# Column pairs 2 and 3 of each FFN's first projection as a Strassen group: ten groups instead of nine

## The chip, the cores and the metric

The kernel runs on one core of one Trainium2 chip. The metric is the device time of one execution in microseconds (us). Before the change three runs gave 1077.87, 1078.4 and 1086.64 us, median 1078.4 us. Stretches of time below are counted from the first instruction of the profiled execution.

## The reference

A two-layer decoder trunk on one sequence of 512 tokens with 1024 channels, all in float32. Each layer is a mixer and then a SwiGLU feed-forward network (FFN), each followed by a residual sum and a layer norm:

```
D_MODEL, SEQ, DEPTH, D_FF = 1024, 512, 2, 2816

def swiglu(x, w_in, w_out):          # w_in 1024 x 5632, w_out 2816 x 1024
    h = x @ w_in
    return (silu(h[..., :D_FF]) * h[..., D_FF:]) @ w_out

for layer in range(DEPTH):
    mix = even_mixer(x, ...) if layer % 2 == 0 else odd_mixer(x, ...)
    x = layer_norm(ALPHA * x + mix, ...)
    x = layer_norm(ALPHA * x + swiglu(x, ffn_w_in[layer], ffn_w_out[layer]), ...)
```

The even mixer is a short gated convolution beside a multi-window pooling, the odd mixer a forgetting attention beside a Conformer convolution; each has one input and one output projection. The change touches the FFN alone.

## The kernel before

**Precision.** Matrices are multiplied in a float32r format. Each operand is split into two: `hi`, a copy in that format made by ScalarE (ACT), and `lo`, the remainder, made by VectorE (DVE) or GpSimd (POOL). A product is then three matmuls, hi·hi, hi·lo and lo·hi (`split` in lines 85 to 88, `mm3` in lines 90 to 93). So every weight block costs a load, one ACT pass and one DVE or POOL pass before TensorE (PE) can use it whole. The activations stand transposed as `xh` and `xl`: 8 blocks of 128 channels by 512 tokens.

**The two forms of the first projection.** Of `w_in`, 22 blocks of 128 gate columns and 22 of 128 up columns are needed. A *plain* block n takes its two column blocks through `project` (lines 151 to 157): 2 column blocks x 8 channel blocks x 3 matmuls of 128x512. `load_cols` fetches 512 KB into a `raw` buffer (3 of them), and hi and lo go into `wt` buffers (8 of them). The blocks n = 0 and 1 (`FIRST = 2`) are loaded together, their lo by POOL, and are computed in two halves of 256 tokens (`SPLIT`), so that the first half runs while the last token blocks are still being normalised. The blocks n = 2 and 3 were plain too (`PLAIN = 4`), each over all 512 tokens.

From column `PLAIN` on, two neighbouring blocks make a *group* (class `Strassen`). It treats channels, tokens and the gate/up choice as 2x2 blocks and needs seven products P1 to P7 instead of eight. A product (lines 383 to 390) is 2 x 4 x 3 = 24 matmuls of 128x256. Its stationary side is a combination of four 512 KB weight quarters `q11, q21, q22, q12`, which `load` (line 364) brings into `wt` buffers in this order; `add` (line 370, DVE) forms the sums S1 to S4; `hi` (line 377, ACT) and `lo` (line 381, DVE) split each of the seven operands into `sw` buffers. The moving side are combinations of the activations that are formed once per FFN.

**`moving`** (lines 319 to 350) forms them on DVE and ACT, outside the fixed part: `less` twice (lines 328 to 330: t3 and t1, each with a help buffer `combl` from `wt`), `minus` twice (lines 334 and 335: t2, t4), and four splits (lines 87 and 88): T2 and T3, t1 back into a block of `xh`/`xl` (so only after the plain matmuls have read that block), and T4. That is ten DVE operations of 128x1024 and four lo's.

**The order in a group** is written by hand (`group`, lines 425 to 485, inside `manual_schedule` for PE, ACT and DVE). PE runs P1, P4 of the group before, P2, P3 of the group before, P6, P5, P7; the first group of a run has no P4 and P3 of another before it. P1 and P2 use `xh`/`xl` as they are, P6 the combination T2, P5 the t1, P7 the T3. `opening` (lines 420 to 423) comes ahead of P1: hi of P1 on ACT, then on DVE the sum S1 = q21 + q22 and only after it the lo of P1. `c1` and `u2`, `u3` (line 397) are copies of PSUM made by ACT. Every wait of an engine holds up what stands behind it on that engine. Outside the hand-written part a scheduler decides the order at build time; the loads all stand on SyncE's (SP) queue in one order, and a load that waits for its buffer holds up those behind it.

**The FFN** (`ffn`, lines 502 to 568): plain blocks, `moving`, the groups up to column 12 (`PART`), the first half of the output projection (`OutProj`), the groups from column 12 to 21 (five of them), and the rest of the output projection with the layer norm. The last group of each run ends in `closing` (lines 487 to 500).

Of the kernel before, what the change touches and what calls it, by code (L numbers as in the profile page):

```python
# [39 lines left out]
FIRSTS = "x0 d1 d2 x1 w0 d3 ww A0 w1 x2 A1 x3 B0 B1 pp"  # L40
SPLIT = [(0, 256), (256, 512)]
FIRST = 2
PLAIN = 4
PART = 12
SHIFT = 16
DFIRST = 2
# [15 lines left out]
def trunk(ctx, tc, x, ev_w_in, ev_conv_w, ev_pool_w, ev_pool_scale, ev_w_out, od_w_in,  # L62
# [131 lines left out]
    def affine_steps(g, b, eng):  # L194

        gb = [wtp.tile([P, D], F32, tag="wt", name="gb") for _ in range(2)]
        for dst, v in zip(gb, (g, b)):
            nc.sync.dma_start(dst, v.partition_broadcast(P))
        return [lambda t=t, cs=slice(c * 512, (c + 1) * 512), v=v, op=op:
                eng.tensor_tensor(xs[t][:, cs], xs[t][:, cs], v[:, cs], op=op)  # L200
                for t in range(NT) for c in range(2) for v, op in zip(gb, (ALU.mult, ALU.add))]
# [300 lines left out]
    def ffn(l):  # L502
        w_in, w_out = ffn_w_in[l], ffn_w_out[l]
        with tc.tile_pool(name=f"ffn{l}", bufs=1) as hp:
# [6 lines left out]
            lhs = lambda k: [y[:, k % 2, :] for y in pairs[k // 2]]  # L511
            for n in range(PLAIN):
                if n < FIRST and n % FIRST == 0:
# [18 lines left out]
            def groups(ns, then=lambda i: None):  # L532

                ns, last = list(ns), None
                load = lambda: st.load(w_in, ns.pop(0), new_pair()) if ns else None
                g = load()
                st.opening(g)
                while g:
                    g, last = st.group(g, last, load, then), g
                st.closing(last)  # L540

            FIXED = {mybir.EngineType.PE, mybir.EngineType.Activation, mybir.EngineType.DVE}
            with tc.manual_schedule(engines=FIXED):
# [5 lines left out]

                groups(range(PLAIN, PART, 2), load_out)  # L550
                steps = affine_steps(ln_mix_g[l], ln_mix_b[l], nc.vector)
# [600 lines left out]
```

## Time and profile before

| | us |
|---|---|
| median of three runs | 1078.4 |
| the profiled execution, its own time | 1077.13 |
| span of the profiled execution | 1075.4 |
| PE busy | 1040.8 |
| DVE busy | 742.5 |
| ACT busy | 482.6 |
| mean granted clock of PE | 0.990 |

The time of the profiled execution is 1.7 us longer than its span. PE is busy in 97% of the span. Rows of the timeline give the start, the length, the engine, the line of the kernel, the operation and its tiles; in square brackets stands how long the engine was idle before and what released it. `x24` means that neighbouring instructions are merged. Matmuls overlap, so that their spacing is read from their starts and not from their lengths.

### The profile page before, as it was taken

The numbers are of one execution on the slowest core, as the hardware profiler recorded it, in microseconds if no ns is written. First come the engines' busy times: TensorE is split into PE (matmuls) and PEld (weight loads), VectorE is DVE, ScalarE is ACT, GpSimd is POOL, SyncE is SP. The second block draws the span as 40 slices with busy tenths as digits, with TensorE's granted clock in tenths as the row PEclk, the third lists the DMA queues.
The fourth block names the chain that finished last, engine by engine and source line by source line (L and its number), as shares of the span: only waits on it lengthen the run. The fifth ranks groups of instructions, "written<-read, shape, count | busy, mean of one in ns | idle before, by whom it ended". The sixth has DMA issues, their size and how long they took to land.

```text
span 1075.4 us, 16367 instructions
## 1 busy us (share of the span) xinstructions
PE 1040.8 (97%) x6649; PEld 934.3 (87%) x6649; DVE 742.5 (69%) x1028; ACT 482.6 (45%) x711; POOL 177.1 (16%) x162
## 2 busy tenths in 40 slices
PE   8999999999799999999999999999999799999997
PEld 8888899899788999988978777889899788999986
DVE  3845476988653788757579978466888663788756
ACT  4433243554321455433576888533555321455420
POOL 1000300000000000012499972710000000000003
PEclk9999999999899999999999999999999899999999
DMA  6523502530423340460333332411530433340522
GB/s 197 148 84 113 157 1 63 174 99 21 157 98 118 119 136 21 137 177 21 80 86 91 96 104 59 121 36 42 183 110 2 163 111 117 118 138 21 164 72 79
DMA packets 112457, 108.49 MB, mean 101 GB/s; under 512 B 5256, under 2 KB 93880, under 8 KB 112382
## 3 DMA queue, kind: packets, MB, share of 16 engines
q1 hardware_dynamic: 110462, 105.35, 31.8%
q10 hardware_dynamic: 1920, 2.10, 0.6%
q8 instruction: 52, 0.85, 0.3%
q14 instruction: 23, 0.19, 0.1%
HBM read 103.17 MB, written 2.10 MB: 98 GB/s over the span
## 4 chain that ended last, share of the span: by engine, by line
PE 76%; DVE 10%; ACT 5%; issue 3%; DMA 2%; POOL 2%; ACTq 0%; SPq 0%; POOLq 0%; DVEq 0%
PE fl L389 13%; PE fl L91 8%; PE fl L93 8%; PE fl L92 8%; PE sc L389 6%; PE sc L93 5%; PE sc L92 5%; PE sc L91 5%; DVE sw L381 4%; DVE sum L370 2%; PE py L92 2%; PE py L91 2%; PE py L93 2%; PE cv L93 2%; PE cv L91 2%
## 5 line engine op out<-in xcount | busy, mean ns | idle before, releaser
L87 ACT ACTIVATE w<-raw 128x1024 fp32r<-128x1024 f32 x104 | 109.4, 1058 | 197.4 <-PE sc L92 64.2
L389 PE MATMUL fl<-T,sw 128*128 128x256 f32 x1296 | 162.0, 281 | 14.2 <-ACT u L397 11.1
L389 PEld LDWEIGHTS fl<-T,sw 128*128 128x128 f32 x1296 | 155.5, 191 | 16.8 <-ACT u L397 12.2
L88 DVE TENSOR_TENSOR w<-raw,w 128x1024 fp32r<-128x1024 f32 x77 | 93.9, 1223 | 84.0 <-ACT w L87 83.4
L88 POOL TENSOR_TENSOR w<-raw,w 128x1024 fp32r<-128x1024 f32 x27 | 64.9, 2415 | 417.9 <-ACT w L87 404.2
L377 ACT ACTIVATE sw<-sum 128x1024 fp32r<-128x1024 f32 x72 | 76.1, 1062 | 102.9 <-DVE sum L370 77.3
L381 DVE TENSOR_TENSOR sw<-sum,sw 128x1024 fp32r<-128x1024 f32 x72 | 87.8, 1219 | 24.7 <-ACT sw L377 24.7
L389 PE MATMUL sc<-xh,sw 128*128 128x256 f32 x576 | 104.5, 277 | 0.0
L389 PEld LDWEIGHTS sc<-xh,sw 128*128 128x128 f32 x576 | 89.7, 188 | 0.1
L381 DVE TENSOR_TENSOR sw<-q,sw 128x1024 fp32r<-128x1024 f32 x54 | 65.4, 1220 | 29.2 <-ACT sw L377 29.1
L389 PE MATMUL sc<-xl,sw 128*128 128x256 f32 x288 | 79.8, 277 | 0.0
L169 POOL TENSOR_TENSOR rs<-rs,neghalf 128x1 f32<-128x1 f32 x20 | 13.6, 678 | 401.8 <-DVE rs L168 401.8
L377 ACT ACTIVATE sw<-q 128x1024 fp32r<-128x1024 f32 x54 | 56.4, 1051 | 44.2 <-DMA q<-in_ffn_w_in 44.2
L91 PE MATMUL fl<-w,hh 128*128 128x512 f32 (+1 forms) x176 | 67.8, 385 | 0.5 <-ACT w L87 0.5
L93 PE MATMUL fl<-w,hl 128*128 128x512 f32 (+1 forms) x176 | 67.6, 384 | 0.0
L92 PE MATMUL fl<-w,hh 128*128 128x512 f32 (+1 forms) x176 | 67.6, 384 | 0.0
L755 DVE SCALAR_TENSOR_TENSOR cv<-hp,par,cv 128x512 f32<-128x512 f32 x84 | 63.1, 751 | 5.8 <-ACT cv L743 4.5
L370 DVE TENSOR_TENSOR sum<-q,q 128x1024 f32<-128x1024 f32 x36 | 43.9, 1218 | 25.5 <-DMA q<-in_ffn_w_in 25.5
L91 PE MATMUL sc<-xh,w 128*128 128x256 f32 (+1 forms) x168 | 55.1, 332 | 0.0
L92 PE MATMUL sc<-xl,w 128*128 128x256 f32 (+1 forms) x168 | 55.0, 329 | 0.0
L389 PE MATMUL fl<-xh,sw 128*128 128x256 f32 x288 | 53.2, 279 | 1.9 <-DVE sw L381 1.9
L93 PE MATMUL sc<-xh,w 128*128 128x256 f32 (+1 forms) x168 | 54.8, 328 | 0.0
(419 smaller groups left out, 2638.8 us busy)
## 6 DMA issues: line engine op xcount, KB each, us to landing
q<-in_ffn_w_in SPq DMA_DIRECT2D x72, 512.0 KB
raw<-in_ffn_w_out SPq DMA_DIRECT2D x44, 512.0 KB
raw<-in_od_w_in SPq DMA_DIRECT2D x20, 512.0 KB
raw<-in_ffn_w_in SPq DMA_DIRECT2D x16, 512.0 KB
raw<-in_ev_w_in SPq DMA_DIRECT2D x15, 512.0 KB
raw<-in_ev_w_out SPq DMA_DIRECT2D x8, 512.0 KB
raw<-in_od_w_out SPq DMA_DIRECT2D x8, 512.0 KB
qk<-qk SPq DMA_DIRECT2D x16, 128.0 KB
```

The source lines that it names most:

```text
L87: nc.scalar.activation(hi, src, AF.Copy)
L88: (eng or nc.vector).tensor_tensor(lo, src, f32(hi), op=ALU.subtract)
L91: nc.tensor.matmul(acc, lh, rh, start=start, stop=False)
L92: nc.tensor.matmul(acc, lh, rl, start=False, stop=False)
L93: nc.tensor.matmul(acc, ll, rh, start=False, stop=stop)
L169: nc.gpsimd.tensor_tensor(rs[:, 1:2], rs[:, 0:1], neghalf, op=ALU.pow)
L370: nc.vector.tensor_tensor(raw[name], raw[a], raw[b], op=ALU.add)
L377: nc.scalar.activation(g["A"][name][0], g["raw"][self.LEFT[name]], AF.Copy)
L381: nc.vector.tensor_tensor(lo, g["raw"][self.LEFT[name]], f32(hi), op=ALU.subtract)
L389: nc.tensor.matmul(acc, l[:, k, cols], r[:, k, :], start=start and i == k == m == 0, stop=stop and i == 1 and k == 3 and m == 2, skip_grou ...
L755: V.scalar_tensor_tensor(acc if i == KCONV - 1 else part, hp[:, i:i + S], tap(i), part, op0=ALU.mult, op1=ALU.add)
```

## The change

One constant: the blocks 2 and 3 of each FFN are no longer plain, and the loop of groups begins at column 2. The first run of groups of an FFN has five instead of four.

```
-PLAIN = 4
+PLAIN = 2

 for n in range(PLAIN):                        # line 512, plain blocks
...
 groups(range(PLAIN, PART, 2), load_out)       # line 550, groups
```

Per FFN, 96 matmuls of 128x512 go and 168 of 128x256 come; four loads of 512 KB from the same columns are replaced by four quarters of 512 KB; four hi's, four lo's, two SiLU-and-multiply steps over 128x512 are replaced by the eleven DVE operations of 128x1024 and seven ACT copies of a group with its gating.

The orders that the scheduler makes differ in three places that matter below, all at the start of FFN 0 (FFN 1 has the same ones). On PE nothing moves ahead of the last matmul of block 1; the 96 rows of 128x512 behind it are gone, and the first group's P1 follows at once.

DVE, from `moving` to the lo of the first group's P1. `comb` are t1 to t4, `T` the splits of T2, T3 and T4, `xl` that of t1, `h` and `hl` the gated output of a plain block and its lo, `sum` here S1, and `sw` the lo of P1. Before:

```order
L330 TENSOR_TENSOR comb<-comb,combl 128x1024 x2
L334 SCALAR_TENSOR_TENSOR comb<-comb,xh 128x1024
L526 TENSOR_TENSOR h<-cv,sg 128x512
L335 TENSOR_TENSOR comb<-comb,xl 128x1024
L88 TENSOR_TENSOR hl<-h,hh 128x512
L88 TENSOR_TENSOR T<-comb,T 128x1024 x2
L334 SCALAR_TENSOR_TENSOR comb<-comb,xh 128x1024
L335 TENSOR_TENSOR comb<-comb,xl 128x1024
L370 TENSOR_TENSOR sum<-q_1713,q_1715 128x1024
L381 TENSOR_TENSOR sw<-q_1711,sw 128x1024
```

and now, from the same `minus` on:

```order
L334 SCALAR_TENSOR_TENSOR comb<-comb,xh 128x1024
L335 TENSOR_TENSOR comb<-comb,xl 128x1024
L88 TENSOR_TENSOR hl<-h,hh 128x512
L526 TENSOR_TENSOR h<-sc,sg 128x512
L88 TENSOR_TENSOR xl<-comb,xh 128x4x256
L88 TENSOR_TENSOR T<-comb,T 128x1024
L88 TENSOR_TENSOR hl<-h,hh 128x512
L334 SCALAR_TENSOR_TENSOR comb<-comb,xh 128x1024
L88 TENSOR_TENSOR T<-comb,T 128x1024
L335 TENSOR_TENSOR comb<-comb,xl 128x1024
L370 TENSOR_TENSOR sum<-q_1575,q_1577 128x1024
L381 TENSOR_TENSOR sw<-q_1573,sw 128x1024
```

The lo of P1 stands behind all of `moving` but the lo of T4, as before; the split of t1 has moved ahead of it.

ACT at the same place. `sg` is the SiLU of a plain block's gate, `hh` the hi of its output, `sw` the hi of P1 (from the first quarter) and of P2 (from the last). Before:

```order
L524 ACTIVATE sg<-py 128x512
L377 ACTIVATE sw<-q_1711 128x1024
L87 ACTIVATE hh<-h 128x512
L87 ACTIVATE T<-comb 128x1024 x2
L524 ACTIVATE sg<-fl 128x512
L377 ACTIVATE sw<-q_1717 128x1024
L87 ACTIVATE xh<-comb 128x4x256
```

and now:

```order
L524 ACTIVATE sg<-fl 128x512
L377 ACTIVATE sw<-q_1573 128x1024
L524 ACTIVATE sg<-sc 128x512
L87 ACTIVATE hh<-h 128x512
L87 ACTIVATE xh<-comb 128x4x256
L87 ACTIVATE T<-comb 128x1024
L87 ACTIVATE hh<-h 128x512
L87 ACTIVATE T<-comb 128x1024
L377 ACTIVATE sw<-q_1579 128x1024
```

The hi of P1, which waits for the first quarter's load, stands ahead of one `sg`, both `hh` and the hi's of `moving`.

SP, the loads of the first quarters with the semaphores they wait for (the numbers at their ends say nothing here). Before:

```order
L98 DMA raw<-in_ffn_w_in 128x8x128 [waits DMAHW5_49,DVE_49]
L364 DMA q_1711<-in_ffn_w_in 128x4x256 [waits DVE_49,PE_49]
L364 DMA q_1713<-in_ffn_w_in 128x4x256 [waits DVE_49,PE_49]
L364 DMA q_1715<-in_ffn_w_in 128x4x256 [waits PE_49,Activation_49]
L364 DMA q_1717<-in_ffn_w_in 128x4x256 [waits PE_49]
```

and now:

```order
L98 DMA raw<-in_ffn_w_in 128x8x128 [waits DMAHW1_49,Pool_49]
L364 DMA q_1573<-in_ffn_w_in 128x4x256 [waits PE_49,Pool_49]
L364 DMA q_1575<-in_ffn_w_in 128x4x256 [waits PE_49]
L364 DMA q_1577<-in_ffn_w_in 128x4x256 [waits DVE_49]
L364 DMA q_1579<-in_ffn_w_in 128x4x256 [waits DVE_49]
```

The first two quarters now take the `wt` buffers of the second plain column block (their PE wait is its last lo·hi matmuls over the second half of the tokens), the third and fourth those of the two help buffers of `less` (their DVE wait is the two rows at line 330).

More of the change, by code (lines that the diff above doesn't have):

```diff
@@ L42 @@
 FIRST = 2
-PLAIN = 4
+PLAIN = 2
 PART = 12
```

## The prediction

> **What bounds the kernel now.** First the page: PE is busy in 97% of the span and holds 76% of the chain that ended last. Anything that takes PE time away helps, anything that makes PE wait hurts at once, and DVE has room only on average.
>
> ```profile
> PE 1040.8 (97%) x6649; PEld 934.3 (87%) x6649; DVE 742.5 (69%) x1028; ACT 482.6 (45%) x711; POOL 177.1 (16%) x162
> PE 76%; DVE 10%; ACT 5%; issue 3%; DMA 2%; POOL 2%; ACTq 0%; SPq 0%; POOLq 0%; DVEq 0%
> ```
>
> Second the table by stretch (length, then busy time of PE, its weight loads, DVE, ACT and POOL), cut at the stages of FFN 0: plain blocks 2 and 3, the first group, the second, the third.
>
> ```profile
> 174.00:195.70 21.70, 21.70 (x98) 17.97 (x97) 18.07 (x18) 9.22 (x11) 0.00 (x0) 1.00 0.47 146
> 195.70:212.20 16.50, 14.56 (x122) 13.91 (x122) 14.77 (x15) 7.21 (x9) 0.00 (x0) 1.00 0.42 128
> 212.20:231.75 19.55, 19.30 (x171) 19.10 (x169) 16.49 (x17) 9.68 (x12) 0.00 (x0) 1.00 0.43 135
> 231.75:250.80 19.05, 19.05 (x171) 19.05 (x170) 16.80 (x17) 10.22 (x14) 0.00 (x0) 1.00 0.09 30
> ```
>
> A settled group fills PE without a gap, and DVE is then 88% busy (16.80 of 19.05). While PE does the plain pair, DVE works for 18.07 of 21.70 us, mostly on `moving` for groups still to come. The plain pair is the cover under which `moving` runs.
>
> Third the timeline of PE at the same place:
>
> ```profile
> 165.45 0.28 PE L92 MATMUL fl<-xl,w 128*128 128x256 f32 x1
> 168.21 0.28 PE L92 MATMUL fl<-xl,w 128*128 128x256 f32 x1
> 173.97 0.40 PE L91 MATMUL py<-xh,w 128*128 128x512 f32 x1
> 174.67 0.40 PE L91 MATMUL py<-xh,w 128*128 128x512 f32 x1
> 195.53 0.39 PE L93 MATMUL fl<-xh,w 128*128 128x512 f32 x1
> 195.76 0.28 PE L389 MATMUL fl<-xh,sw 128*128 128x256 f32 x1
> 196.62 0.51 PE L389 MATMUL fl<-xh,sw 128*128 128x256 f32 x2 [0.46 <-DVE sw L381]
> 202.84 0.50 PE L389 MATMUL fl<-T,sw 128*128 128x256 f32 x2 [0.73 <-ACT sw L377]
> 204.10 2.79 PE L389 MATMUL fl<-T,sw 128*128 128x256 f32 x22 [0.76 <-DVE sw L381]
> 209.45 2.88 PE L389 MATMUL fl<-T,sw 128*128 128x256 f32 x24
> 212.17 0.28 PE L389 MATMUL fl<-xh,sw 128*128 128x256 f32 x1
> ```
>
> The first two rows are the last lo matmuls of the first and of the second plain column block; the plain pair starts at 173.97, P1 of the first group at 195.76, P1 of the second at 212.17.
>
> **The PE work removed and added.** From 174.67 (the fourth of the pair's 96 matmuls) to 195.53 (the last) are 92 steps: 0.2267 us each, 96 of them 21.8 us (173.97 to 195.76 says the same). A product is 24 matmuls in 212.17 - 209.45 = 2.72 us, 0.1133 us each, and seven are 19.05 us, the length of the third group. So where nothing waits a group saves 21.77 - 19.05 = 2.72 us per FFN, an eighth of the pair.
>
> Here a rule speaks against the change. The Trainium skill, "TensorE: Matmul & The Clock Gate", section "Back-to-back issue gap", gives about 131 ns for a sustained matmul of 512 columns and 81 ns for one of 128; in between, 256 columns would be an estimated 98 ns, the pair 12.6 us and the group 16.4 us, and the change would add 3.8 us per FFN instead of saving 2.72, which makes the sum below 1103 us. The same kinds of instruction at 227 and 113 ns in this trace decide against it.
>
> **The opening of the first group.** Its five products took 212.17 - 195.76 = 16.41 us against 5 x 2.72 = 13.60: 2.81 us of waits. What will they be when P1 stands at 173.97? P1's first two matmuls need the hi of P1 (ACT), the third its lo (DVE). DVE and its steps, before:
>
> ```profile
> 160.54 0.69 DVE L88 TENSOR_TENSOR xl<-xt,xh 128x512 fp32r<-128x512 f32 x1 [0.16 <-ACT xh L87]
> 179.41 2.36 DVE L329 TENSOR_TENSOR combl<-xl 128x1024 f32<-128x1024 f32 x2 [1.61 <-PE py L92]
> 181.69 2.35 DVE L330 TENSOR_TENSOR comb<-comb,combl 128x1024 f32<-128x1024 f32 x2
> 185.22 0.68 DVE L526 TENSOR_TENSOR h<-cv,sg 128x512 f32<-128x512 f32 x1
> 185.82 1.21 DVE L335 TENSOR_TENSOR comb<-comb,xl 128x1024 f32<-128x1024 f32 x1
> 191.81 1.23 DVE L334 SCALAR_TENSOR_TENSOR comb<-comb,xh 128x1024 f32<-128x1024 f32 x1
> 193.06 1.23 DVE L335 TENSOR_TENSOR comb<-comb,xl 128x1024 f32<-128x1024 f32 x1
> 194.21 1.22 DVE L370 TENSOR_TENSOR sum<-q,q 128x1024 f32<-128x1024 f32 x1
> 195.34 2.35 DVE L381 TENSOR_TENSOR sw<-q,sw 128x1024 fp32r<-128x1024 f32 x2
> ```
>
> A 128x1024 operation takes 1.14 us start to start (179.41 to 181.69 is two) and 1.22 to its end, 1.25 where it needs the one ahead of it (191.81 to 193.06); one of 128x512 takes 0.60.
>
> `combl` waits for a buffer that the first plain column block gives up. In the changed order nothing of PE moves ahead of that: its last lo matmul starts at 165.45 and ends 0.28 later. So line 329 starts at 165.76, line 330 at 168.04 and 169.18, and the first `minus` at 170.92 behind the `h` at 170.32; its second step runs from 172.17 to 173.39. Next is `hl`, which needs an `hh` from ACT, and ACT now has the hi of P1 and with it a load ahead of that. The loads as SP issues them, the first and the fourth quarter:
>
> ```profile
> 183.00 0.37 SPq L364 DMA_DIRECT2D q<-in_ffn_w_in  x1
> 185.32 0.50 SPq L364 DMA_DIRECT2D q<-in_ffn_w_in  x1
> ```
>
> and ACT, which uses them:
>
> ```profile
> 186.84 1.06 ACT L377 ACTIVATE sw<-q 128x1024 fp32r<-128x1024 f32 x1 [6.54 <-DMA q<-in_ffn_w_in]
> 187.81 0.61 ACT L87 ACTIVATE hh<-h 128x512 fp32r<-128x512 f32 x1
> 188.33 2.00 ACT L87 ACTIVATE T<-comb 128x1024 fp32r<-128x1024 f32 x2
> 192.45 1.06 ACT L377 ACTIVATE sw<-q 128x1024 fp32r<-128x1024 f32 x1 [1.27 <-DMA q<-in_ffn_w_in]
> 199.49 0.60 ACT L397 ACTIVATE c<-fl 128x512 f32<-128x512 f32 x1 [4.09 <-PE fl L389]
> ```
>
> The first quarter was issued at 183.00 and used at 186.84: 3.84 us. The fourth, behind three others, took 185.32 to 192.45: 7.13 us. These are the bounds for the new load; I take 3.84, since it is again the first of its four on an idle queue. It waits for the lo matmul of 168.21, is issued at 168.55 and lands at 172.39. ACT then does hi of P1 (172.39), `sg` (173.36) and `hh` (173.86 to 174.48), with the steps of 0.97 and 0.5 shown. So DVE starts `hl` at 174.55, `h` at 175.15, the lo of t1 at 175.75, of T2 at 176.89, `hl` at 178.03, `minus` at 178.63, the lo of T3 at 179.77, `minus` at 180.91, S1 at 182.05 and the lo of P1 at 183.19, done at 184.41. ACT's hi's are ahead of each of these by then, and the quarters for S1 are there at 7.13 us too (176.5). PE, which has done two matmuls of P1, waits from 174.20 to 184.47: **10.27 us**, and behind it waits everything, since the order of PE is fixed.
>
> **The clock after the wait.** The trace has two waits of more than 5 us, at the end of each first run of groups:
>
> ```profile
> 275.83 4.57 PE L389 MATMUL fl<-T,sw 128*128 128x256 f32 x24 [5.53 <-ACT u L397]
> 280.24 0.28 PE L389 MATMUL sc<-xh,sw 128*128 128x256 f32 x1
> 273.00:274.00 1.00, 0.00 (x0) 0.50 0.66 246
> 842.34 4.59 PE L389 MATMUL fl<-T,sw 128*128 128x256 f32 x24 [5.57 <-ACT u L397]
> ```
>
> In the wait the granted clock falls to 0.50 (third row), and the product behind it takes 280.24 - 275.83 = 4.41 us instead of 2.72: **1.69 us** lost. After 10.27 us I expect the same: the other 22 matmuls of P1 need 2.49 + 1.69 and end at 188.65. Bounds: nothing, or two such losses.
>
> The Trainium skill, "TensorE: Matmul & The Clock Gate", section "What's actually happening", has the clock halved after an idle window of about 3.4 us and freed after a busy one, with windows that run on regardless of the kernel; half a clock for one window is an estimated 1.7 us, as measured, but a wait that ends inside a window could leave the next one slow too (the last rival).
>
> **The rest of the opening.** P2 runs from 188.65 to 191.37. `c1` starts behind P1's end (0.25 us after it, 188.9), the hi of P6 behind `c1` at 189.4, its lo at 190.5 to 191.73: P6's third matmul waits 0.2 us, and P6 ends at 194.29. The lo's of P5 and P7 are done at 193.5 and 197.0, P5 and P7 run without a gap, and P1 of the second group starts at 199.73, with the lo of its own late by about 0.5, as at 212.17 before.
>
> **The sum.** Per FFN the opening lasts 199.73 - 173.97 = 25.76 us, with 12.16 us of waits instead of 2.81: +9.35. With -2.72 that is **+6.63 us**. FFN 1 has the same order, and the trace shows the same spacing there (plain pair to second group 38.05 us, against 38.20):
>
> ```profile
> 740.58 0.40 PE L91 MATMUL fl<-xh,w 128*128 128x512 f32 x1
> 778.63 0.28 PE L389 MATMUL fl<-xh,sw 128*128 128x256 f32 x1
> 490.00:740.00 250.00, 242.34 (x1465) 208.69 (x1464) 183.80 (x376) 158.56 (x315) 145.86 (x112) 0.99 0.26 75
> ```
>
> So +13.3 us on the profiled execution's own 1077.1: 1090.4. The median of the runs is 1.3 us above that execution; I put 1091. Costed at nothing: the loads (as many bytes as before; DMA's share is 0.47 in the pair's stretch, the last column but one), the gating of the new group (inside the settled group's DVE load of 88%), and the scheduler's small shifts among ACT, DVE and POOL in the odd mixer. The last is unknown: PE idles 7.7 us there in all (last row), so it could gain or lose a few; I take 0 and keep 3 us each way for the range.
>
> **The rivals.**
> *A shorter opening, within 1%.* If the clock did not fall, or `moving` ran about 1.7 us ahead of my walk, each FFN costs 4.9 us: 1087. For it: DVE is idle just ahead (161.2 to 165.8) and the walk adds up waits of ACT. Against: both long waits of the trace show the slow clock.
> *DVE keeps up, not slower.* If the opening's waits stayed at 2.81 us, only the saving were left: 1077.1 - 5.4 = 1071.7. It decides when the waits stay below 2.81 + 2.72 = 5.53 us, that is, when P1's lo is done by about 178 instead of 184.4. For it: the two first subtractions of `moving` can now run in DVE's idle time after 161.2. Against: line 329 waits for PE's 165.45, and behind it stand 16 operations up to P1's lo, some 16 us of DVE work.
> *The load lands late.* `hh` hangs on the first quarter. With 7.13 us instead of 3.84 the chain behind it moves by 3.3 us: 1097.
> *The clock stays low for a second stretch*: another 1.69 us per FFN, 1094.
>
> **How the numbers follow.** About 1% (10.8 us) is what a measurement of this kernel tells from no change. My forecast has 0.60, the shorter opening 0.20, DVE keeping up 0.05, the late load 0.08, the second slow stretch 0.07. Slower by over 1%: 0.60 + 0.08 + 0.07, less a little for a forecast that ends just under the line, 0.73. Within 1%: the two short cases and that little, 0.25, since 1071.7 is within it too. Faster by over 1%: 0.02. The range runs from the shorter opening less the odd mixer's 3 us, 1084, to the late load, 1097; DVE keeping up and combined mishaps lie outside.
>
> **What would show it.** Right: twice a wait of about 10 us on PE at line 389 that DVE's `sw` of line 381 ends, P1 of the second group at about 199.7, the clock at 0.5 in that wait, the rest of P1 in 4.2 us, and in the list of waits "PE fl L389 <- DVE sw L381" at 22 to 25 us; settled groups still 19.05 us. Wrong: P1 released by ACT or a DMA instead, the first quarter landing much after 172.4, a wait below 6 us, or a change of more than 2 us between the FFNs.

## The result, and the profile after

| kernel | median of the runs | all of them | profiled execution, its span |
|---|---|---|---|
| before, nine groups | 1078.2 us (6 runs) | 1077.5 to 1086.6 | 1077.1 us, 1075.4 |
| changed, ten groups | 1095.5 us (6 runs) | 1093.9 to 1096.9 | 1095.7 us, 1094.0 |

The ratio is 1.0149 with a 95% interval of 1.0117 to 1.0180: slower by about 1.5%. The two profiled executions differ by 18.5 us (their spans by 18.6), against 13.3 in the sum of the prediction.

The page of the changed kernel: PE has about as much work as before (1041.7 us against 1040.8) in a longer span, so its share falls from 97% to 95%.

```profile
PE 1041.7 (95%) x6793; PEld 943.1 (86%) x6793; DVE 760.5 (70%) x1046; ACT 490.6 (45%) x721; POOL 177.2 (16%) x162
PE 75%; DVE 11%; ACT 5%; issue 4%; POOL 2%; DMA 2%; ACTq 0%; SPq 0%; POOLq 0%; DVEq 0%
```

Where the time went is read from landmarks on PE's timeline: the end of the first plain pair (173.81 and 747.56 now, one step behind the last lo matmul; 173.97 and 740.58 before) and the first matmuls of the output projections:

```profile
292.19 0.40 PE L91 MATMUL fl<-w,hh 128*128 128x512 f32 x1
449.49 0.50 PE L91 MATMUL fl<-w,hh 128*128 128x512 f32 x1 [0.38 <-ACT w L87]
747.44 0.28 PE L93 MATMUL fl<-xh,w 128*128 128x256 f32 x1
866.38 0.40 PE L91 MATMUL fl<-w,hh 128*128 128x512 f32 x1
1025.46 0.50 PE L91 MATMUL fl<-w,hh 128*128 128x512 f32 x1
```

The same places before were at 283.06, 440.58, 740.58, 849.49 and 1006.91.

| stretch | before | after | difference |
|---|---|---|---|
| start to the end of FFN 0's first plain pair | 173.97 | 173.81 | -0.16 |
| FFN 0: from there to its output projection | 109.09 | 118.38 | **+9.29** |
| to FFN 0's second output projection | 157.52 | 157.30 | -0.22 |
| odd mixer, to the end of FFN 1's first pair | 300.00 | 298.07 | -1.93 |
| FFN 1: from there to its output projection | 108.91 | 118.82 | **+9.91** |
| to FFN 1's second output projection | 157.42 | 159.08 | +1.66 |
| to the end | 68.49 | 68.54 | +0.05 |

So the loss stands in the two stretches that the change touches. The table by stretch cuts the first of them into the opening (to the second group's P1), the second and the third group; the fourth row is the opening in FFN 1. Columns as in the prediction; the last but two is the granted clock.

```profile
173.81:201.04 27.23, 16.78 (x123) 16.42 (x121) 21.33 (x21) 13.00 (x17) 0.00 (x0) 0.75 0.48 149
201.04:220.76 19.72, 19.32 (x170) 19.12 (x169) 16.67 (x17) 9.67 (x12) 0.00 (x0) 1.00 0.42 132
220.76:239.80 19.04, 19.04 (x170) 19.04 (x169) 16.80 (x17) 10.21 (x14) 0.00 (x0) 1.00 0.37 111
747.56:775.48 27.92, 16.18 (x122) 15.52 (x121) 21.37 (x21) 13.88 (x17) 0.00 (x0) 0.76 0.47 147
```

The settled group takes 19.04 us, as before. Both openings are long: PE is busy for 16 to 17 us of 27 to 28, DVE for 21.3. PE's timeline shows the place (FFN 0, then FFN 1):

```profile
174.05 0.38 PE L389 MATMUL fl<-xh,sw 128*128 128x256 f32 x1
184.92 0.58 PE L389 MATMUL fl<-xh,sw 128*128 128x256 f32 x1 [10.37 <-DVE sw L381]
189.78 0.41 PE L389 MATMUL py<-xh,sw 128*128 128x256 f32 x1
192.77 0.28 PE L389 MATMUL fl<-T,sw 128*128 128x256 f32 x1
201.04 0.28 PE L389 MATMUL fl<-xh,sw 128*128 128x256 f32 x1
...
749.67 0.39 PE L389 MATMUL fl<-xh,sw 128*128 128x256 f32 x1 [1.95 <-ACT sg L524]
760.05 0.58 PE L389 MATMUL fl<-xh,sw 128*128 128x256 f32 x1 [9.78 <-DVE sw L381]
764.30 0.28 PE L389 MATMUL py<-xh,sw 128*128 128x256 f32 x1
775.48 0.28 PE L389 MATMUL fl<-xh,sw 128*128 128x256 f32 x1
```

P1 starts, does two matmuls and then waits some 10 us for its lo (line 381). In FFN 1 it waits first for `sg`, which nothing in the prediction names. ACT and SP of both FFNs tell why:

```profile
172.94 1.06 ACT L377 ACTIVATE sw<-q 128x1024 fp32r<-128x1024 f32 x1 [6.61 <-DMA q<-in_ffn_w_in]
174.38 0.62 ACT L87 ACTIVATE hh<-h 128x512 fp32r<-128x512 f32 x1
748.07 1.06 ACT L377 ACTIVATE sw<-q 128x1024 fp32r<-128x1024 f32 x1 [7.99 <-DMA q<-in_ffn_w_in]
749.03 0.58 ACT L524 ACTIVATE sg<-fl 128x512 f32<-128x512 f32 x1
```

```profile
168.41 7.63 SPq L364 DMA_DIRECT2D q<-in_ffn_w_in  x8
742.15 8.77 SPq L364 DMA_DIRECT2D q<-in_ffn_w_in  x8
```

The first load was issued at 168.41 and used at 172.94 (4.53 us), in FFN 1 at 742.15 and 748.07 (5.92 us). ACT works in order: behind the hi of P1, which waits for that load, stand `sg` and `hh`. P1's bank in FFN 1 (`fl`) is that of the third accumulator, and it comes free only when `sg` has read it. On DVE the walk of the prediction is seen step by step:

```profile
165.61 2.36 DVE L329 TENSOR_TENSOR combl<-xl 128x1024 f32<-128x1024 f32 x2 [2.27 <-PE fl L92]
172.01 1.23 DVE L335 TENSOR_TENSOR comb<-comb,xl 128x1024 f32<-128x1024 f32 x1
175.03 0.69 DVE L88 TENSOR_TENSOR hl<-h,hh 128x512 fp32r<-128x512 f32 x1 [1.79 <-ACT hh L87]
183.65 2.35 DVE L381 TENSOR_TENSOR sw<-q,sw 128x1024 fp32r<-128x1024 f32 x2
750.16 0.69 DVE L88 TENSOR_TENSOR hl<-h,hh 128x512 fp32r<-128x512 f32 x1 [3.18 <-ACT hh L87]
```

From line 329 on DVE stops once, for `hh` (1.79 and 3.18 us), and then works without a gap up to P1's lo. The list of waits sums it up (us in total, times, the longest):

```profile
PE fl L389 <- DVE sw L381: 21.4, 6, 10.4
PE fl L389 <- ACT sg L524: 1.9, 1, 1.9
```

### The profile page after: what moved, and what is told of

Read it like the earlier page. It is cut to its first block, busy times and chain, and to the rows that moved or that the text cites. A ratio compares the mean times of both kernels' runs of the same rounds, so it can differ in the third digit from the quotient of the medians.

```text
span 1094.0 us, 16682 instructions
## 1 busy us (share of the span) xinstructions
PE 1041.7 (95%) x6793; PEld 943.1 (86%) x6793; DVE 760.5 (70%) x1046; ACT 490.6 (45%) x721; POOL 177.2 (16%) x162
## 4 chain that ended last, share of the span: by engine, by line
PE 75%; DVE 11%; ACT 5%; issue 4%; POOL 2%; DMA 2%; ACTq 0%; SPq 0%; POOLq 0%; DVEq 0%
PE fl L389 14%; PE fl L91 8%; PE fl L93 8%; PE fl L92 8%; PE sc L389 6%; DVE sw L381 5%; PE sc L91 4%; PE sc L92 4%; PE sc L93 4%; DVE sum L370 3%; PE py L91 2%; PE py L93 2%; PE py L92 2%; PE cv L91 2%; PE cv L92 2%
## 5 line engine op out<-in xcount | busy, mean ns | idle before, releaser
L389 PE MATMUL fl<-T,sw 128*128 128x256 f32 x1440 | 181.3, 282 | 11.3 <-ACT u L397 10.8
L389 PEld LDWEIGHTS fl<-T,sw 128*128 128x128 f32 x1440 | 174.4, 192 | 13.5 <-ACT u L397 12.0
L88 DVE TENSOR_TENSOR w<-raw,w 128x1024 fp32r<-128x1024 f32 x69 | 83.9, 1222 | 73.7 <-ACT w L87 72.9
L381 DVE TENSOR_TENSOR sw<-sum,sw 128x1024 fp32r<-128x1024 f32 x80 | 97.5, 1219 | 31.9 <-ACT sw L377 31.9
L389 PE MATMUL sc<-xh,sw 128*128 128x256 f32 x640 | 116.8, 278 | 0.0
L389 PEld LDWEIGHTS sc<-xh,sw 128*128 128x128 f32 x640 | 99.9, 188 | 0.1
L389 PE MATMUL fl<-xh,sw 128*128 128x256 f32 x320 | 63.3, 292 | 23.2 <-DVE sw L381 21.1
L389 PEld LDWEIGHTS fl<-xh,sw 128*128 128x128 f32 x320 | 53.0, 200 | 25.4 <-DVE sw L381 22.5
L389 PEld LDWEIGHTS sc<-xl,sw 128*128 128x128 f32 x320 | 60.2, 188 | 0.1
L370 DVE TENSOR_TENSOR sum<-sum,q 128x1024 f32<-128x1024 f32 x40 | 48.7, 1218 | 0.0
```

The source lines that it names most:

```text
L88: (eng or nc.vector).tensor_tensor(lo, src, f32(hi), op=ALU.subtract)
L370: nc.vector.tensor_tensor(raw[name], raw[a], raw[b], op=ALU.add)
L381: nc.vector.tensor_tensor(lo, g["raw"][self.LEFT[name]], f32(hi), op=ALU.subtract)
L389: nc.tensor.matmul(acc, l[:, k, cols], r[:, k, :], start=start and i == k == m == 0, stop=stop and i == 1 and k == 3 and m == 2, skip_grou ...
```

## Experiments

The theory at this point: in each FFN the plain pair was the cover for `moving`; without it P1's lo stands at the end of DVE's chain, PE waits for it, and the clock is halved behind the wait. The rivals: the load and ACT's order are the cause, not DVE's work; a group costs more on PE than a plain pair; the loss sits somewhere else in the program. All runs were timed beside the kernel before; the table gives the ratio to it, and from each profile the two stretches from the end of the first plain pair to the output projection. The ratio is to the runs of the kernel before that were taken at the same time: their median was 1078.2 us beside the changed kernel and e1 to e4, 1078.4 beside e5 and e6, 1080.1 beside e7 to e10, and the single run beside e11 and e12 took 1082.2. Lines of a diff that are not code name an engine and its order in words, and `...` marks what is left out.

| run | median us | ratio to before (95%) | FFN 0 | FFN 1 |
|---|---|---|---|---|
| before | 1078.2 | | 109.09 | 108.91 |
| changed | 1095.5 | 1.0149 (1.0117 to 1.0180) | 118.38 | 118.82 |
| e1 change in FFN 0 alone | 1086.8 | 1.0067 (1.0041 to 1.0094) | 117.68 | 109.86 |
| e2 ACT's order | 1093.0 | 1.0127 (1.0106 to 1.0147) | 115.63 | 116.07 |
| e3 PE kept busy | 1094.2 | 1.0133 (1.0111 to 1.0156) | 116.44 | 117.39 |
| e4 without `moving` | 1075.2 | 0.9969 (0.9954 to 0.9985) | 105.74 | 108.65 |
| e5 P1 and P2 first | 1097.3 | 1.0175 (1.0156 to 1.0194) | 118.07 | 118.51 |
| e6 and GpSimd helps | 1092.7 | 1.0135 (1.0114 to 1.0156) | 117.15 | 117.03 |
| e7 e5 with `u2` ahead | 1089.8 | 1.0089 (1.0067 to 1.0110) | 113.78 | 117.48 |
| e8 by what PE needs next | 1090.4 | 1.0095 (1.0077 to 1.0114) | 113.84 | 114.22 |
| e9 nine groups, `combl` early | 1076.9 | 0.9968 (0.9953 to 0.9982) | 107.10 | 107.97 |
| e10 e9 and P6's hi early | 1077.1 | 0.9978 (0.9966 to 0.9990) | 107.93 | 107.55 |
| e11 the changed kernel again | 1098.5 (1 run) | | 117.13 | 121.35 |
| e12 e9 again | 1074.3 (1 run) | | 108.33 | 108.71 |

**e1: the change in one FFN.**

```diff
+        plain = 4 if l else PLAIN
-            for n in range(PLAIN):
+            for n in range(plain):
-                groups(range(PLAIN, PART, 2), load_out)
+                groups(range(plain, PART, 2), load_out)
```

> The change in FFN 0 alone; FFN 1 keeps its two plain column pairs and nine groups in all. Theory (the loss is made separately in each FFN, where moving loses the cover of the plain pair): the trace of the changed kernel has FFN 0 longer by 9.3 us from the end of the first plain pair to the output projection, FFN 1 by 9.9 in the same stretch; so this kernel takes 1078.2 + 9.3 = 1087.5 us, up to 2 us less if the odd mixer's gain of 2 us comes along. In FFN 0 a wait of about 10.4 us at P1, in FFN 1 none over 1 us before the closing one. Rival (the loss is one cost of another schedule, shared by the program, or sits mostly in FFN 1): 1078 to 1081 or above 1092.

Measured: 1086.8 us, where 1087.5 was expected; FFN 0 longer by 8.6 us, with the same wait, FFN 1 by 0.95:

```profile
185.13 0.58 PE L389 MATMUL fl<-xh,sw 128*128 128x256 f32 x1 [10.37 <-DVE sw L381]
```

The loss is made in each FFN by itself, and half the change makes half of it.

**e2: ACT's order.** The tails of the two plain blocks, `moving` and P1's operands are written out by hand in the order that DVE had anyway; only ACT's hi of P1 moves.

```diff
-ACT: sg(0), hi of P1, sg(1), hh(0), hi of t1, of T2, hh(1), hi of T3, of P2, ...
+ACT: sg(0), hh(0), sg(1), hi of t1, of T2, hh(1), hi of T3, hi of P1, of P2, ...
```

> Ten groups. The only edit: ACT turns P1's first quarter (hi of P1, which waits for its load) behind sg, hh and the hi's of moving instead of ahead of them; DVE's order is the same, instruction by instruction. Theory (DVE's chain is stretched by 1.8 us in FFN 0 and 3.2 us in FFN 1 because hh stands behind a load on ACT): PE's wait at P1 ends about 1.2 us earlier in FFN 0 and about 2.7 us earlier in FFN 1 (hh then hangs on h and the last plain matmul), and the 1.95 us wait of P1's first matmul for sg in FFN 1 goes: 1095.5 - 3.9 = 1091.6 us. Rival (DVE's own work is the bound, the gap on it is filled anyway): 1095.5, no change. Rival (the late load is the main cause): below 1086.

Measured: 1093.0 us, where 1091.6 was expected. The third matmul of P1 now starts 9.56 us behind the end of the plain pair in FFN 0 (174.08 to 183.64) and 9.56 in FFN 1 (746.97 to 756.53), instead of 11.11 and 12.49:

```profile
177.65 0.58 PE L400 MATMUL fl<-xh,sw 128*128 128x256 f32 x1 [3.41 <-ACT sw L388]
183.64 0.58 PE L400 MATMUL fl<-xh,sw 128*128 128x256 f32 x1 [5.19 <-DVE sw L392]
...
756.53 0.58 PE L400 MATMUL fl<-xh,sw 128*128 128x256 f32 x1 [5.19 <-DVE sw L392]
```

With `hh` free of the load the two FFNs are equal to the hundredth, so what set them apart was the load's landing, and it cost 1.5 and 2.9 us. (P1's first matmul now waits 3.41 us for its hi; that costs nothing, since the lo decides.) The other 9.6 us are DVE's own: in FFN 0 it works from line 329 (165.88) to behind P1's lo with one gap of 0.24 us.

**e3: the clock.** Surplus matmuls ahead of P1, which write a bank that nobody reads.

```diff
+            if not last and self.busy:
+                bank = tpsum()
+                for _ in range(self.busy):
+                    nc.tensor.matmul(bank[:, :256], xh[:, 0, :P], xh[:, 0, :256], start=True, stop=True)
+                self.busy = 0
             self.product(g, "P1", g["x"], start=True)
```

> Ten groups, and ahead of P1 of the first group PE does 90 (FFN 0) and 100 (FFN 1) matmuls of 128x256 that nobody reads, 10.2 and 11.3 us of work at full clock, so that it does not stand idle while it waits. Theory (behind the wait the clock is halved; it cost 2.6 us in FFN 0, where 46 matmuls took 7.85 us instead of 5.2, and 1.8 us in FFN 1): the wait still ends when DVE's lo is done, but P1 and P2 run at 0.1133 us a matmul: 1095.5 - 4.4 = 1091.1 us. Rival (the slow matmuls behind the wait are not the clock but late operands): 1095.5. Rival (the surplus matmuls end later than the lo and delay P1): above 1095.5.

Measured: 1094.2 us, where 1091.1 was expected; the medians alone don't tell it from no change. The openings do: 25.21 and 26.00 us instead of 27.23 and 27.92, 3.9 us less together. In FFN 0 P1 still waits for the lo, but 0.19 us instead of 10.37, and what follows runs at 0.1133 us a matmul:

```profile
185.27 0.38 PE L390 MATMUL fl<-xh,sw 128*128 128x256 f32 x1 [0.19 <-DVE sw L382]
```

So the slow matmuls behind the wait were the clock, and the lo is there no sooner. Of these 3.9 us, 2.6 are left between the two profiled executions (1093.06 against 1095.67 us); the rest went at other places, FFN 1's first run of groups and the odd mixer (see e11 on what such differences are worth).

**e4: without `moving`.**

```diff
-            st.moving()
+            st.B = {p: st.block(*ij) for p, ij in dict(P1=(0, 0), P2=(1, 0), P3=(1, 1), P4=(0, 0), P5=(0, 1),
+                                                       P6=(1, 0), P7=(1, 1)).items()}
```

> Ten groups, but the combinations of moving are left out: P4 to P7 multiply plain blocks of x (as many matmuls of the same shapes), so the output is another one. Theory (the whole loss is moving on DVE with nothing to cover it; without it the ten groups give the saving of 2.72 us per FFN): PE waits 2 to 4 us in each opening for the first load, S1 and the lo's, against 2.8 before, and the time is about 1078.2 - 5.4 + 1 = 1074 us (1071 to 1077). Rival (a group costs more on PE than the plain pair that it replaces, whatever DVE does): 1084 or more. Rival (the first load's late landing is the bound): 1080 to 1086.

Measured: 1075.2 us, where 1074 was expected, and 20 us below the changed kernel with the same ten groups on PE. P1 waits 0.83 us in FFN 0 and 1.86 in FFN 1; PE's timeline, and the row of the table by stretch for FFN 0's opening, which is over at 189.2:

```profile
175.37 0.39 PE L389 MATMUL fl<-xh,sw 128*128 128x256 f32 x1 [0.83 <-DVE sw L381]
...
743.20 0.39 PE L389 MATMUL fl<-xh,sw 128*128 128x256 f32 x1 [1.86 <-DVE sw L381]
```

```profile
174.15:190.00 15.85, 14.75 (x125) 14.15 (x124) 13.66 (x15) 8.78 (x12) 0.00 (x0) 1.00 0.66 209
```

This speaks for the theory against both rivals: the groups' PE work is no dearer than the plain pair's, and the whole loss hangs on `moving`, on its DVE work and on what comes with it (without its help buffers the first load is issued at 165.94 instead of 168.41, and ACT makes the hi of P1 at 169.94 instead of 172.94; e2 has the price of that part). One reason why FFN 1 gains less than FFN 0 is another: behind its wait of only 1.86 us the clock was at half (0.50 from 744 to 747), and P1 took 6.48 us, 1.90 more than its 2.72 and the wait.

**e5 to e8: can the tenth group be covered in another way?** P1 and P2 need nothing of `moving`. e5 puts their operands ahead of the parts that P5, P7 and P4 need (t1 to t4 are the combinations of `moving`; H and L are a hi and its lo, l1 to l7 the lo's of the operands of P1 to P7, S1 to S4 the sums, h and hl as above, a and b the two steps of a `minus`; an apostrophe marks the second group):

```diff
-... t2a t2b hl0 h1 t1L t2L hl1 t4a t3L t4b S1 l1 l2 t4L ...
+... t2a t2b hl0 l1 t2L h1 S1 l2 hl1 S2 l6 t1L l5 t3L S3 l7 t4a t4b S4 S1' l1' ...
+ACT: ... t4H (waits for t4b) silu u2 ...
```

> Ten groups, the same work on every engine, but in the first group the operands of P1 and P2 (hi and lo of the first and fourth quarter, S1), which need nothing of moving, stand ahead of the parts of moving that only P5, P7 and P4 need; those parts follow behind the lo's of P6, P5 and P7. Theory (PE waits because P1's lo stands last in DVE's chain; what must be ahead of P6 is only the first 10 of the 16 operations): P1 waits about 1.5 us for its lo, P6 starts near 182.5 us instead of 192.8, the second group's P1 near 194 instead of 201; some 7 us less per FFN, 1095.5 - 14 = 1082 us, that is still 4 us above the nine groups, because DVE has the same sum of work. Rival (the order within the chain does not matter, DVE's sum decides): P1 early, but the second group near 200 and 1093 to 1096. Rival (the first load decides): P1 starts after 176 and the time is about 1086.

Measured: 1097.3 us, where 1082 was expected: no gain. P6 was early as expected (its first matmuls at 182.96), but then P7 waited:

```profile
196.27 0.58 PE L407 MATMUL fl<-T,sw 128*128 128x256 f32 x1 [6.41 <-ACT u L415]
```

ACT shows that it was the placing of one instruction in this kernel, the hi of T4 ahead of `silu` and `u2`:

```profile
194.16 1.06 ACT L356 ACTIVATE T<-comb 128x1024 fp32r<-128x1024 f32 x1 [3.69 <-DVE comb L348]
195.12 0.61 ACT L425 ACTIVATE g<-g 128x512 f32<-128x512 f32 x1
195.64 0.58 ACT L415 ACTIVATE u<-fl 128x512 f32<-128x512 f32 x1
```

e6 has the same placing, with T3's split and the two `hl` earlier, and lets `combl` use the gate tiles and GpSimd do four of the lo's:

```diff
-                t = wtp.tile([P, 4, 256], F32, tag="wt", name="combl")
+                t = self.hp.tile([P, 2 * S], F32, tag="g", name="combl", bufs=2)...
-            nc.vector.tensor_tensor(lo of T3, T4, hl0, hl1, ...)
+            nc.gpsimd.tensor_tensor(lo of T3, T4, hl0, hl1, ...)
```

> Ten groups with the order of the run before, and three covers more: the two buffers of combl come from the gate tiles, which are free then, so that DVE need not wait for the first plain column block and the four loads are issued one column block earlier; and GpSimd, which is idle, does the lo's of T3, T4 and of the two plain blocks (4 operations of the 16, 3.5 us of DVE time). Theory (the tenth group's saving of 2.72 us per FFN is real once DVE's chain is off PE's path): DVE starts line 329's work 2.3 us earlier, P1 follows the plain blocks without a wait, P6 waits less than 1 us, the second group's P1 starts near 189 to 191 us; about 4 us per FFN less than the nine groups: 1070 us (1067 to 1076). Rival (DVE's sum of work still binds, and the debt comes out at the second group or behind it): 1077 to 1083. Rival (GpSimd's operations slow DVE's beside them): 1078 or more, with DVE's 128x1024 operations above 1.14 us a step.

Measured: 1092.7 us, where 1070 was expected; P7 waited 5.28 us for `u2`, so that the run can't show what the two other covers are worth. It answers the question on GpSimd all the same:

```profile
168.04 2.41 POOL L358 TENSOR_TENSOR T<-comb,T 128x1024 fp32r<-128x1024 f32 x1 [14.61 <-ACT T L356]
168.62 0.69 DVE L553 TENSOR_TENSOR h<-fl,sg 128x512 f32<-128x512 f32 x1 [0.67 <-PE fl L95]
169.23 2.31 DVE L345 SCALAR_TENSOR_TENSOR comb<-comb,xh 128x1024 f32<-128x1024 f32 x1
```

DVE's operation of 169.23 took 2.31 us instead of 1.22: until GpSimd's ends at 170.45 and then about its usual time. The Trainium skill, "SBUF — State Buffer", section "SBUF: two separate sides", has the two engines share one pair of ports under a lock that the one holds for its whole instruction while the other is stopped; the row agrees. So an operation handed to GpSimd saved DVE 1.14 us and cost it 1.09. The next, `hl` in 1.50 us, saved it 0.60 and cost it 0.99 (DVE's operation of 171.57 took 2.21 us); FFN 1 has the same two. DVE's operation of 168.62, which has one input in PSUM, took its usual 0.69 us beside GpSimd.

e7 is e5 with that one hi of T4 behind `u2`:

```diff
-LEFT = "P6: t1L t3H;P5: t3L;P7: t4a t4b t4H;P4: t4L"
+LEFT = "P6: t1L t3H;P5: t3L;P7: t4a t4b;P4: t4H t4L"
```

> The run e5 with one instruction moved: ACT's hi of T4, which waits for the last step of moving on DVE, stands behind the copy u2 and the next group's hi instead of ahead of silu and u2. Theory (in e5 P7 waited 6.41 us in each FFN for u2, which stood behind that hi on ACT, and ran at half clock behind the wait; the order of P1 and P2 itself gains): the 6.4 us wait goes, P7 waits about 1 us for its own lo, the second group's P1 waits some 4 us for its lo at the end of DVE's debt, and the time is 1097.3 - 2 x 7 = 1083 us (1080 to 1087), as was expected of e5. Rival (DVE's sum decides whatever ACT does): the wait only moves to the second group's P1 and the time stays above 1091.

Measured: 1089.8 us, 7.5 less than e5 where 14 were expected, and between the ranges of theory and rival. P7's wait fell to 1.67 us (1 was expected), and the second group's P1 waited 2.81 in FFN 0 and 2.80 in FFN 1 (4 expected); the openings last 20.3 and 21.3 us instead of 27.2 and 27.9. The two equal waits had unequal costs: in FFN 0 that product took 5.82 us, 0.29 beyond the wait and 2.72, in FFN 1 7.42 us, 1.90 beyond, for there the clock was at half behind it:

```profile
769.20:772.50 3.30, 3.30 (x18) 3.30 (x17) 3.30 (x5) 0.00 (x0) 0.00 (x0) 0.50 0.47 156
```

e8 leaves GpSimd out, orders DVE by what PE needs next, and puts P4 of the first group behind P2 of the second and P3 of the first:

```diff
+... t2a t2b l1 t2L h0 S1 hl0 l2 S2 t1L l6 h1 l5 S3 t3L l7 S4 S1' l1' hl1 l2' u3 l3 t4a t4b t4L l4 ...
-PE, second group: P1, P4 of the first, P2, P3 of the first, P6, ...
+PE, second group: P1, P2, P3 of the first, P4 of the first, P6, ...
```

> Ten groups; GpSimd does none of the work; combl in the gate tiles as in e6; DVE's order in the first two groups is by what PE needs next: lo of P1, lo of T2, S1, lo of P2, S2, lo of P6, lo of P5, S3, lo of T3, lo of P7, S4, then the second group's S1 and lo of P1, and T4 with all that hangs on it last; in the second group P4 of the first comes behind P2 and P3 instead of ahead of them (the order of three products of PE), so that DVE has 5.4 us more for T4. Theory (with moving's parts each ahead of its use the tenth group pays its 2.72 us per FFN, and the opening waits 2.8 us of before shrink too): waits of 0.3, 0.7, 0.6 and 0.2 us at P1, P7, the second P1 and P4, about 3 us per FFN less than nine groups: 1072 us (1069 to 1077). Rival (DVE's debt of some 5 us beside a load of 88 per cent comes out as a wait later in the second or third group): 1077 to 1084. Rival (ten groups cost more anyway): above 1086.

Measured: 1090.4 us; missed by 18, and in the range of the second rival. The openings are as short as planned (16.9 and 17.8 us, below the 19.1 at which ten groups break even), but the debt came out behind them, which is the mechanism of the first rival, at a higher price than it gave. The first three groups:

```profile
173.91:235.75 61.84, 55.77 (x459) 53.58 (x457) 52.87 (x53) 31.14 (x39) 0.00 (x0) 1.00 0.41 128
```

The stretch holds 19 products, 51.7 us at 2.72 each, and lasts 61.84: eleven waits of 0.27 to 1.68 us (6.1 us in all), the longest at P6 of the second group, and some 4 us more. The kernel before needed 57.78 us for the plain pair and two groups, to the same point. DVE is busy for 52.87 us here, 85%: most of its idle time lies in steps where a lo waits for its hi on ACT. Each short wait cost PE some 0.28 us beside its own length (P1 of the second group in the changed kernel: 3.40 us with a wait of 0.40, where 2.72 + 0.40 = 3.12), which my estimate left out; eleven of them make about 3 of the 4 us, and the last products ran at 2.83 us instead of 2.72. That a better order exists is not excluded; I found none.

**e9 and e10: the cover for nine groups.** e9 makes the edit on `combl` in the kernel before, and nothing else; e10 also has P6's hi ahead of `c1` in the first group:

```diff
+            if not last:
+                self.hi(g, "P6")
             self.copy(g, "c1", "h")
...
-            self.hi(g, "P6")
+            if_last(lambda: self.hi(g, "P6"))
```

> Nine groups (the kernel before) with one edit: combl takes the two gate tiles, which are free then, instead of two buffers that the first plain column block must give up, so that moving can start some 16 us earlier on DVE. If the opening of nine groups too is bound by DVE's chain, P1's wait (0.46 us for its lo) goes and about 0.7 us per FFN with it; P6's two waits stay, since its hi stands behind the copy c1 on ACT and that behind P1 on PE: 1077 us. Rival (P6 also waits for DVE's chain): 1073. Rival (nothing of the opening hangs on moving's start, the late loads set it): 1078, no change. The scheduler's other order in the odd mixer may add or take 2 us; the two FFNs are read from the trace.

> As the run before, and in the first group ACT makes the hi of P6 ahead of the copy c1 instead of behind it. If P6's two waits (0.73 us for its hi and 0.76 for its lo, and some 0.3 us of refilling behind each) come from c1, which waits for the end of P1, they go: 1.5 to 2.1 us per FFN more than the run before, 1073.5 us (1072 to 1076). With it the nine groups would have the whole opening covered, and take about as little as the ten groups without moving (1075.2). Rival (S2 on DVE is late as well): as the run before.

Measured: 1076.9 and 1077.1 us, where 1077 and 1073.5 were expected, ratios of 0.9968 and 0.9978, both below 1 by more than their intervals: e9 is faster than both kernels, by 0.3% and, by the medians, 1.7%. But e9 gained in another way than was expected: P6's two waits did not stay. In place of 0.73 and 0.76 us there is one of 0.26 us in FFN 0 and one of 0.46 in FFN 1:

```profile
202.42 2.86 PE L389 MATMUL fl<-T,sw 128*128 128x256 f32 x22 [0.26 <-DVE sw L381]
```

So most of P6's wait hung on DVE's chain, as the first rival had it: DVE forms S2, from which P6's hi is made, at 197.20 here and at 200.49 in the kernel before. The openings lasted 14.66 and 14.86 us instead of 16.41 and 16.26. In e10 the opening has no wait left. Five products in 14.14 us:

```profile
195.86:210.00 14.14, 14.14 (x122) 14.13 (x121) 11.96 (x13) 6.97 (x9) 0.00 (x0) 1.00 0.50 150
```

P6's remaining wait came from `c1`, as was expected, but there was little left of it: e10's openings are 0.5 and 0.7 us shorter than e9's, not 1.5 to 2, and the medians don't show that. Both runs took 2.83 us a product in these openings instead of 2.72, which is 0.5 us each.

**e11 and e12: what belongs to the program.** The changed kernel and e9 once more, without an edit.

> The changed kernel itself once more, with a profile, to see what belongs to the program and what to one execution. The waits of the openings (10.4 us in FFN 0; 1.95 and 9.8 us in FFN 1), the half clock behind them and the odd mixer's 217.9 us belong to the program if they come again within 0.3 us. The stretches in which 24 matmuls of 256 columns take 2.83 instead of 2.72 us at a granted clock of 1.00 (from 262 us, and from 860 to the end) belong to the program if they come at the same places; if they lie elsewhere, they belong to the execution, and the 1.7 us that the second run of groups in FFN 1 lost is not the change's.

> The same for the nine groups of e9, which ran its opening of FFN 0 at 2.83 us a product from the first product on. If that is the execution, the opening now takes some 13.6 to 14 us without waits (2.72 a product) at least in one of the two FFNs, or the slow stretches lie elsewhere; if it is the program (no wait, so the slow rate), the products of both openings take 2.83 us again.

The waits are the program's:

```profile
184.91 0.58 PE L389 MATMUL fl<-xh,sw 128*128 128x256 f32 x1 [10.37 <-DVE sw L381]
761.47 0.58 PE L389 MATMUL fl<-xh,sw 128*128 128x256 f32 x1 [9.89 <-DVE sw L381]
```

The half clock behind the waits did not come again within 0.3 us: in e11 it lasted 3.7 us in FFN 0 (184.91 to 188.6) and 4.0 in FFN 1 (761.47 to 765.5), against 5.2 and 3.5 in the execution above. Where the products run at which rate changes too. FFN 1's second run of groups by operation (durations: least, median, most), first in the changed kernel as profiled above, then in e11:

```profile
L389 PE MATMUL sc<-xh,sw x144: 281/281/281, 940.3 to 1022.5; 128*128 128x256 f32 x144
```

```profile
L389 PE MATMUL sc<-xh,sw x143: 276/276/281, 944.0 to 1023.8; 128*128 128x256 f32 x143
```

The same program at the same place runs at 2.83 us a product in one execution and 2.72 in the next; in e11 it was FFN 1's first run of groups instead that was slow (121.35 us), and in e12 FFN 0 ran at 2.72 behind its first two products. The start of an opening is another matter. P1 and P2 took 2.83 us in both openings of e12, as in both of e9 and of e10, and so did P1 in FFN 0 of e8 and FFN 1 of e3; these are all the openings whose P1 has no wait. There the slow rate came with the program each time, which is the other branch of what was expected of e12. Within an execution the rate goes over many products and changes where the even step of the matmuls is interrupted: in e10 from 2.83 to 2.72 at the second group's P1 (a wait of 0.25 us at 210), in e12's FFN 0 at P6's wait of 0.52 us; P6's wait of 0.39 us in its FFN 1 changed nothing. What decides it is not shown. The odd mixer, too: 217.87 us from FFN 0's second output projection to its own in the profile after, 220.21 in e11, 219.80 before. Differences as large as the +1.66 and the -1.93 of the table by stretch thus come without any change, and these two need not be the change's.

## Why the prediction came out as it did

The mechanism was the predicted one, and the forecast was 4.5 us short (1091 against 1095.5; the prediction's own terms, 1090.4 and 1.3, make 1091.7). The terms that were too small are the first load and with it the wait, the clock, and the stretch behind the opening. By its steps:

- *The PE work* (-2.72 us per FFN): settled groups of 19.04 us say the group's size, and e4 that the ten groups are no dearer; that part was right.
- *The opening's walk*: line 329 predicted at 165.76 and found at 165.61, the second step of the first `minus` at 172.17 and 172.01, the load issued at 168.55 and 168.41; the frame of the changed execution is 0.16 us early. Behind `hh` DVE ran its operations up to P1's lo in the order and without the gaps of the walk.
- *The first load*, 3.84 us taken out of 3.84 to 7.13: mis-sized. It was 4.53 us in FFN 0 and 5.92 in FFN 1. Since `hh` hangs on it through ACT's order, the wait ended 11.11 and 12.49 us behind the plain pair instead of 10.50. The chance given to the late load (0.08, at 7.13 us) was the right place at the wrong size; e2 shows the link.
- *P1's first matmul*: FFN 1's 1.95 us for `sg` was not foreseen. "FFN 1 has the same order" was true of the instructions and not of the banks. It cost nothing by itself, being inside the wait for the lo.
- *The clock*, 1.69 us per wait: 2.64 us in FFN 0 (46 matmuls from 184.92 to 192.77, 7.85 us against 5.21) and 1.76 in FFN 1 (760.05 to 767.02). In FFN 0 half clock lasted to 190.1, 5.2 us behind the wait, in FFN 1 to 763.6, 3.5 us (the last column but two of the rows below, for one us each). That is part of the rival of a second slow stretch, in one of the two FFNs.

```profile
189.00:190.00 1.00, 1.00 (x7) 1.00 (x7) 0.00 (x0) 0.00 (x0) 0.00 (x0) 0.50 0.00 0
190.00:191.00 1.00, 1.00 (x9) 1.00 (x9) 0.00 (x0) 0.92 (x2) 0.00 (x0) 0.94 0.00 0
762.00:763.00 1.00, 1.00 (x7) 1.00 (x7) 1.00 (x2) 0.00 (x0) 0.00 (x0) 0.50 0.00 0
763.00:764.00 1.00, 1.00 (x8) 1.00 (x8) 0.41 (x1) 0.00 (x0) 0.00 (x0) 0.72 0.00 0
```

  The Trainium skill, "TensorE: Matmul & The Clock Gate", section "What's actually happening", has windows of 3.4 us that run on regardless of the kernel, of which one busy one frees the clock; a stretch of between one and two windows is what that would give, and 3.5 and 5.2 us agree, as do the 3.7 and 4.0 of e11. So the size of this term is partly chance. Nor does the clock need a wait of 3.4 us to fall, as the prediction had it: 1.86 us (e4, FFN 1) and 2.80 us (e7, FFN 1) were enough, where 2.81 us (e7, FFN 0) was not.
- *The rest of the opening*: P6's wait of 0.2 us did not come, the second group's lo was late by 0.40 instead of 0.5. Openings of 27.23 and 27.92 us against 25.76: +1.47 and +2.16.
- *Behind the opening* the prediction had one group of 19.05 us more. Measured were 20.26 (70.89 to 91.15 from the second group to the output projection) and 20.04: 1.0 to 1.2 us more per FFN. In FFN 0 some of it is the slow rate in the last products ahead of the closing wait, which e11 and e12 show at other places in other executions; the rest is not explained.
- *Costed at nothing*: the odd mixer moved by -1.93 us inside the 3 us allowed, but need not have done so through the scheduler, as the prediction thought: between its output projections it is 217.87 us here and 220.21 in e11 with the same program. That it nearly cancels the +1.66 of FFN 1's second run of groups, and so leaves the forecast 4.5 us off and the range intact, is luck.

Together, against +6.63 per FFN: FFN 0 +1.47 +1.21 = 9.31 (measured 9.29), FFN 1 +2.16 +0.99, and 0.15 for its shorter stretch before, 9.93 (measured 9.91).

Of what the text said would show it, the wait of 10 us by DVE's lo came twice, the clock was at 0.5, and the FFNs agree within 2 us. The rest of P1 took 4.86 and 4.25 us (4.2 foretold), the second group's P1 stood at 201.0 (199.7), and the line of the list of waits at 21.4 us (22 to 25), as PE's wait in FFN 1 is split between `sg` and the lo. Of the signs of being wrong one came in part: in FFN 1 ACT's `sg` released P1's first matmul, and the load landed 2.1 us later than the walk had it.

What stays open: why the load took 5.92 us in FFN 1 and 4.53 in FFN 0, what sets the two rates of the products, and what the 1.0 us behind FFN 1's opening are.

## What to carry to other kernels

A cheaper form of work on the busiest engine can be a loss where the old form was the cover for another engine's chain: before replacing it, list what that engine does meanwhile and for whom. If an operand stands at the end of an in-order queue, look at what is ahead of it that PE does not need yet, and at loads that a neighbour's queue waits for; but count the sum of the work too, for here no order that I tried made room for 16 us of DVE work beside groups that load DVE to 88%. A plan that leaves many short waits pays for each of them twice, for the wait and for some 0.28 us behind it. Compare stretches between landmarks of two profiles rather than medians when the effect is of a few us, and profile one program twice before explaining a difference of 2 us.

## What the runs showed of the hardware

- Matmuls of 128x256 have two rates at a granted clock of 1.00: 24 in 2.72 or in 2.83 us (276 or 281 ns each in the records), in stretches of tens of us that lie elsewhere in another execution of the same program. From one output projection to the next, over the five groups between, FFN 1 took 159.08 us with its products at the slow rate (the changed kernel) and 157.48 with most at the fast one (e12). All eight openings whose P1 has no wait began at the slow rate.
- Behind waits of 10 us PE ran at half clock for 3.5 to 5.2 us (the changed kernel and e11). A wait of 2.81 us left the products behind it at full clock (e7, FFN 0), one of 2.80 us (e7, FFN 1) and one of 1.86 us (e4, FFN 1) did not: these cost 1.90 us beyond the wait. The same wait can thus cost differently in the two FFNs.
- A short wait that leaves the clock at full costs PE some 0.28 us more than the wait (P1 of the second group: 0.28 behind 0.40 us in the changed kernel, 0.29 behind 2.81 us in e7).
- A 128x1024 operation of GpSimd (2.41 us) held up DVE's two-input operation beside it by 1.09 us, about what it had saved; one of 128x512 (1.50 us) held up the next by 0.99 and saved 0.60 (e6).
